# All of x transposed by TensorE in a hybrid attention encoder, with its first eight steps written out by hand

## The chip, the core and the metric

One core of one Trainium2 chip runs the whole layer. The metric is the device time of one execution in microseconds (us); the time given for a kernel is the median of its runs.

## What is computed

One layer for x of 1024 tokens by 1024 features, float32: a root-mean-square norm, one projection to 3328 columns, two groups of attention heads on its parts, a gate for each, an output projection, the residual, and a final norm. Cut to what matters:

```python
h = _rmsnorm(x, norm_gain[l])
proj = h @ w_in[l]
q_a, k_a, v_a, g_a, q_b, k_b, v_b, g_b = jnp.split(proj, split_at, axis=-1)
q_a = _rmsnorm(q_a.reshape(b, s, A_HEADS, HEAD_DIM), q_norm_a[l])      # 8 heads of 64
k_a = _rmsnorm(k_a.reshape(b, s, A_KV_HEADS, HEAD_DIM), k_norm_a[l])   # 2 heads
q_a = q_a * cos + _rotate_half_axial(q_a) * sin
k_a = k_a * cos + _rotate_half_axial(k_a) * sin
o_a = _gqa_blocked(q_a, k_a, v_a) * jax.nn.silu(g_a)      # softmax over all 1024 keys
o_b = _neighbourhood_attn(q_b, k_b, v_b, na_rpb[l]) * jax.nn.silu(g_b)   # window 8 x 16 of the 16 x 64 grid
x = x + jnp.concatenate([o_a, o_b], axis=-1) @ w_out[l]
return _rmsnorm(x, final_norm_gain)
```

## The kernel before

**Precision.** The matrix products run in float16, each operand split into a high part and the rest (hi and lo), and three products are summed: hi·hi, hi·lo, lo·hi. So each projection of one tile of 128 tokens to 256 columns has 8 chunks of the contraction times 3, 24 matmuls.

**The work on PE.** The tokens are 8 tiles (u = 0 to 7). The columns are groups of 256: group 0 (KVA) is K and V of head group A, 1 and 2 (QA) are its Q, 3 to 12 the rest, 13 to 16 the output projection. `proj_pair` (L511) makes the projection of one group for two tiles, a *pair* of 48 matmuls in 8 *chunks* of 6; its left operand comes from hT, the transposed x, in hi (`hT[0]`) and lo (`hT[1]`). Nine pairs come before the first score of group A, in the order K0 Q0 K1 Q1 K2 K3 Q2 Q3 (each number is two tiles) and the first of group 2. Then 64 *units* follow, one for each Q tile and head: scores (L741, L743), their softmax on DVE and ACT (L748, L752, L753, L758), a DMA transpose of the probabilities (L763), and five units later the product with V (L775, L776). The projections still to be done fill PE between, at 5.0 chunks a unit for the first four units and 4.2 for the next seven. Group B's attention and the output projection come behind.

**How x gets into hT.** For each tile: `load_x` (L234) brings it in, into one of four buffers; `x_sq` (L298) sums its squares on ACT (the last on DVE); `x_rs` (L308) makes the scale (DVE, then two operations on POOL); `x_y` (L314) scales it on DVE and copies it on ACT to float16 (the hi part), and `x_lo` (L319) subtracts, on DVE (once on POOL), for the lo part. `x_t` (L323) sends each part through a DMA transpose on SP's queue, so there are 16. For each weight, `prep_a` sums squares, `prep_b` (L382) makes a scale with a small matmul, `prep_c` (L394, ACT) and `prep_d` (L399, DVE) split it; weights from group 3 on are split in quarters (`split`, L408, lines 414 and 419).

**What sets the order.** PE's order is the program's own. The other engines have their order written out by hand in the first part of the program (up to the first `fl.step`); behind it, up to the seventh unit, a scheduler orders them, and then by hand again. `Flow` is a clock of steps: `at(delay, pos, fn)` puts work at a position of a later step, `run(pos)` does what is due there, and `step(n)` runs "pre", "mid" and "post" and then lets PE do n chunks (8 before the first unit). After a pair is projected, `norm_rope` (L537) does its norm and rotation in three pieces: a (ACT, two evacuations of PSUM, L550 and L551), b (DVE sum, POOL power), c (DVE and POOL, the rotation; lines 560 to 568); then `fin` splits the result into hi (ACT) and lo (DVE), and a DMA transpose puts it into kTa and klo1 (K) or qTa (Q).

Of the kernel before, what the change touches and what calls it, by code (L numbers as in the profile page):

```python
# [8 lines left out]
F32 = mybir.dt.float32  # L9
F16 = mybir.dt.float16  # L10
BF16 = mybir.dt.bfloat16
AF = mybir.ActivationFunctionType
# [20 lines left out]
X2_BEHIND = {0: (0, 1), 1: (2,), 2: (3,), 3: (4,), 4: (5,), 5: (6,), 6: (7,)}  # L33
PREP = {2: 4, 3: 0, 4: 2}
NEG = -1.0e37
# [12 lines left out]
class Flow:  # L48
# [78 lines left out]
    def step(self, n, first=None, second=None, last=None):  # L127
        if self.base:
            us = self.base[0] + 0.654 * n
            self.budget = {"act": us - self.base[1], "dve": us - self.base[2]}  # L130
        self.run("pre")
        self.work("act", self.early)
        if first:
            first()
        if self.early is not None:
            self.tail = self.slot
            self.work("act", more=True)
            self.tail = -1
        if second:
            second()  # L140
        self.run("mid")
        self.work("dve")
        self.run("post")
        self.fill(n)
        if last:
            last()
        self.run("end")
        self.slot += 1
# [3 lines left out]
def kernel(ctx: ExitStack, tc: tile.TileContext, x: bass.AP, w: bass.AP, wo: bass.AP,  # L152
# [161 lines left out]
    def x_y(u):  # L314
        dve.scalar_tensor_tensor(xts[u], xts[u], xr[u][:, 1:], gain, op0=OP.mult, op1=OP.mult)
        act.activation(xhl[u][:, 0], xts[u], AF.Copy)
        x_t(u, 0)

    def x_lo(u, e):  # L319
        e.tensor_tensor(xhl[u][:, 1], xts[u], xhl[u][:, 0], op=OP.subtract)  # L320
        x_t(u, 1)
# [71 lines left out]

    def prep_c(g):  # L394
        for i in range(0, KC, KC // 2):
            s = slice(i, i + KC // 2)
            act.activation(wp[g][0][:, s], raw[g][:, s], AF.Copy, scale=col(S_ + g))
# [68 lines left out]
    def prep(g):  # L466
        if g < 3:
            d = PREP.get(g, 1)
            at(d + 1, "pre", prep_a, g)
            at(d + 2, "mid", pend.append, g)  # L470
        else:
            want.add(g)
            try_split(g)
# [61 lines left out]
    klo1 = carve(rq, 16384, [NU, P], F16)  # L535

    def norm_rope(g, up, src, nh, kq, done):  # L537
        n = 2 * nh
# [30 lines left out]

        at(1, "pre", a)  # L570
        at(1, "post" if g == QA + 1 else "mid", b)
        at(2 if g == QA + 1 else 1, "post", c)
        done(qn)

    def qa_gen(hh, up):
        def evac(pt):
            g = QA + hh
            stg = slot("stg1", [P, 2, 4, P], F16)
            a, b = (0, D) if hh == 0 else (D, 0)

            def fin(q):
                d = 4 if hh else 2
# [6 lines left out]
                at(d, "post", tr)  # L589
            norm_rope(g, up, pt, 4, 0, fin)  # L590
        yield from proj_pair(QA + hh, up, from_h, evac)

    def kva_gen(up):
        def evac(pt):
            both = slot("stg1", [P, 8, P], F16)
            stg, stg_l = both[:, :6].rearrange("p (i a) b -> p i a b", a=3), both[:, 6:]
            vs = pt[:, :, P:].rearrange("p a (h d) -> p a h d", d=D)
            at(1, "pre", lambda: act.activation(va[:, 2 * up:2 * up + 2, :, :D], vs, AF.Copy, scale=2.0 ** -14))
# [5 lines left out]
            at(1, "mid", vlo)  # L604

            def fin(k):
                def hi():
                    act.activation(stg[:, :, :2, :D], k, AF.Copy)
                    act.activation(stg[:, :, :2, D:], k, AF.Copy)
                at(2, "pre", hi)  # L610

                def lo():
                    for h, to in ((0, stg[:, :, 2]), (1, stg_l)):
                        dve.tensor_tensor(to.rearrange("p i (e d) -> p i e d", d=D),
                                          k[:, :, h, None, :].to_broadcast([P, 2, 2, D]),
                                          stg[:, :, h].rearrange("p i (e d) -> p i e d", d=D), op=OP.subtract)
                at(2, "mid", lo)

                def tr():
                    sp.dma_start_transpose(kTa[:, 2 * up:2 * up + 2].rearrange("p i a t -> p (i a) t"),  # L620
                                           both[:, :6].rearrange("p a b -> p (a b)"))
                    sp.dma_start_transpose(klo1[:, 2 * up:2 * up + 2], stg_l.rearrange("p a b -> p (a b)"))
                at(2, "post", tr)
            norm_rope(KVA, up, pt[:, :, :P], 2, 1, fin)
# [440 lines left out]
    with tc.manual_schedule(engines={act.engine, dve.engine, pool.engine, sp.engine}):  # L1065
        x_sq(0, act)
        scale_gain()
        prep_a(0)
        load_w1(2, 3)
        x_rs(0)  # L1070
        x_y(0)
        prep_a2(0)
        prep_b(0)
        x_sq(1, act)
        prep_c(0)
        x_rs(1)
        load_x(2)
        x_lo(0, dve)
        x_y(1)
        load_x(3)  # L1080
        prep_a(1)
        x_lo(1, pool)
        prep_d(0)
        tables_in()
        x_sq(2, act)
        load_x(4)
        x_rs(2)
        load_x(5)
        prep_e(0)
        x_sq(3, act)  # L1090
        x_y(2)
        x_rs(3)
    k, q = [kva_gen(up) for up in UP], group(1, [qa_gen(0, up) for up in UP])
    fl.add(k[0], q[0], k[1], q[1], k[2], k[3], q[2], q[3], *group(2, [qa_gen(1, up) for up in UP]))
    fl.step(PAIR)
    prep_b(1)
    prep_c(1)
    x_y(3)
    x_lo(3, dve)
    x_sq(4, act)  # L1100
    tables()
    scale_tab(2)
    x_rs(4)
    x_y(4)
    x_lo(4, dve)
    x_lo(2, dve)
    x_sq(5, act)
    x_rs(5)
    load_x(6)
    scale_tab(0)  # L1110
    x_y(5)
    prep_d(1)
    x_sq(6, act)
    x_lo(5, dve)
    x_rs(6)
    x_y(6)
    x_lo(6, dve)
    load_x(7)
    scale_tab(3)
    x_sq(7, dve)  # L1120
    prep_e(1)
    gate[2] = 6
    scale_tab(1)
    x_rs(7)
    x_y(7)
    load_w(2)
    gate[3] = 5
    x_lo(7, dve)
    load_w(3)

    for p in range(8):
        fl.step(PAIR)
    fl.add(*group(3, [qb_gen(0, up) for up in UP]))
# [214 lines left out]
```

## Time and profile before

| | |
|---|---|
| time, median of 3 runs | 555.65 us (553.15 to 557.3) |
| profiled execution | 554.79 us, span 553.0 us |
| mean granted clock of TensorE | 0.989 |
| PE busy | 507.8 us, 92% of the span |
| DVE, ACT, POOL busy | 445.3 (81%), 381.4 (69%), 178.9 us (32%) |
| first score matmul (L741) | 87.15 us |
| DMA | 95.40 MB, 173 GB/s; 235,489 of 244,509 packets under 512 B |

The execution's own time holds 1.8 us outside of the span. PE is the engine with the most work; its matmuls are pipelined, so a busy PE need not be at its peak. The profile's slices are 13.8 us each.

### The profile page before, as it was taken

The numbers are of one execution on the slowest core, as the hardware profiler recorded it, in microseconds if no ns is written. First come the engines' busy times: TensorE is split into PE (matmuls) and PEld (weight loads), VectorE is DVE, ScalarE is ACT, GpSimd is POOL, SyncE is SP. The second block draws the span as 40 slices with busy tenths as digits, with TensorE's granted clock in tenths as the row PEclk, the third lists the DMA queues.
The fourth block names the chain that finished last, engine by engine and source line by source line (L and its number), as shares of the span: only waits on it lengthen the run. The fifth ranks groups of instructions, "written<-read, shape, count | busy, mean of one in ns | idle before, by whom it ended". The sixth has DMA issues, their size and how long they took to land.

```text
span 553.0 us, 12864 instructions
## 1 busy us (share of the span) xinstructions
PE 507.8 (92%) x5071; PEld 397.2 (72%) x5071; DVE 445.3 (81%) x887; ACT 381.4 (69%) x671; POOL 178.9 (32%) x201
## 2 busy tenths in 40 slices
PE   2657889998999999999999999999999998799994
PEld 0446768876887555558888888988777786589883
DVE  4599678889987888879879898867898997887732
ACT  4545465967887868787787696648688788784411
POOL 1385787581110000101000022634433123344510
PEclk9989999999999999999999999999999999999998
DMA  8997837879999999999997999744897799979722
GB/s 243 210 203 216 146 59 181 135 144 176 208 196 217 191 231 186 216 176 178 194 217 143 202 186 200 120 125 71 146 191 138 136 250 202 219 115 204 173 74 76
DMA packets 244509, 95.40 MB, mean 173 GB/s; under 512 B 235489, under 2 KB 236001, under 8 KB 242530
## 3 DMA queue, kind: packets, MB, share of 16 engines
q1 hardware_dynamic: 242434, 81.23, 80.1%
q0 software_dynamic: 1728, 12.58, 7.3%
q8 instruction: 39, 0.64, 0.5%
q10 hardware_dynamic: 288, 0.79, 0.5%
q14 instruction: 20, 0.16, 0.1%
HBM read 29.56 MB, written 4.19 MB: 61 GB/s over the span
## 4 chain that ended last, share of the span: by engine, by line
PE 50%; DVE 10%; ACT 9%; issue 5%; DMA 3%; POOL 0%; DVEq 0%; POOLq 0%; ACTq 0%
PE pj L504 17%; PE kb L504 7%; PE pjb L504 7%; PE pv L775 5%; PE s L741 4%; PE s L743 4%; ACT rq L856 3%; DVE ar L854 3%; ACT ar L858 2%; PE pv L776 2%; PE sb L504 2%; DMA pt<-ar 2%; DVE ar L863 1%; DMA ar<-ar 1%; DVE whl L419 1%
## 5 line engine op out<-in xcount | busy, mean ns | idle before, releaser
L504 PEld LDWEIGHTS <-hT 128*128 128x128 f16 x2112 | 204.2, 99 | 59.5 <-DMA hT<-ar 16.3
L504 PE MATMUL pj<-whl,hT 128*128 128x256 f16 x1680 | 201.7, 278 | 21.8 <-DMA hT<-ar 9.4
L752 ACT ACTIVATE ar<-s,nm,sm 128x1024 f32<-128x1024 f32 x64 | 76.9, 1201 | 47.7 <-DVE nm L748 45.7
L748 DVE CUSTOM_DVE_ANT_0 ar<-s,sm 128x1024 bf16<-128x1024 f32 x64 | 82.0, 1281 | 30.3 <-PE s L743 28.5
L504 PEld LDWEIGHTS <-ar 128*128 128x128 f16 x768 | 73.8, 98 | 16.0 <-issue 7.8
L758 DVE TENSOR_TENSOR ar<-ar 128x1024 f16<-128x1024 f32 x64 | 79.4, 1241 | 1.2 <-ACT ar L753 1.2
L753 ACT ACTIVATE ar<-ar 128x1024 f16<-128x1024 f32 x64 | 67.6, 1057 | 2.3 <-DVE ar L758 0.4
L504 PE MATMUL pjb<-whl,ar 128*128 128x256 f16 x480 | 56.4, 273 | 2.8 <-ACT whl L414 1.5
L856 ACT ACTIVATE rq<-ar,nm 128x384 f32<-128x384 f32 (+1 forms) x64 | 34.0, 579 | 25.7 <-DVE nm L854 25.1
L504 PE MATMUL pjb<-whl,hT 128*128 128x256 f16 x432 | 50.4, 273 | 0.1
L784 POOL TENSOR_TENSOR ar<-ar,sum 128x256 f32<-128x256 f32 x16 | 11.3, 709 | 110.7 <-DVE ar L783 95.3
L504 PE MATMUL kb<-hT,whl 128*128 128x512 f16 x192 | 44.5, 379 | 0.0
L419 DVE SCALAR_TENSOR_TENSOR whl<-raw,sm,whl 128x512 f16<-128x512 f32 x52 | 41.0, 821 | 2.7 <-ACT whl L414 2.7
L775 PE MATMUL pv<-va,ar 128*128 128x128 f16 x384 | 39.1, 220 | 0.0
L863 DVE SCALAR_TENSOR_TENSOR ar<-rq,ar 128x768 f16<-128x768 f32 (+1 forms) x32 | 29.3, 915 | 11.0 <-ACT ar L858 10.6
L741 PE MATMUL s<-kTa,rq 128*128 128x512 f16 x128 | 38.1, 379 | 0.0
L776 PE MATMUL pv<-va,ar 128*128 128x64 f16 x384 | 37.8, 193 | 0.0
L775 PEld LDWEIGHTS <-ar 128*128 128x128 f16 x384 | 33.9, 98 | 5.3
L776 PEld LDWEIGHTS <-ar 128*128 128x128 f16 x384 | 33.2, 98 | 5.3
L414 ACT ACTIVATE whl<-raw,sm 128x512 f16<-128x512 f32 x52 | 34.0, 709 | 1.4 <-POOL sm L391 1.4
L391 POOL TENSOR_TENSOR sm<-wss,mh 128x1 f32<-128x1 f32 x17 | 10.5, 619 | 72.7 <-DVE wss L390 72.7
L910 POOL TENSOR_TENSOR ar<-ar,qkg 128x256 f32<-128x256 f32 x16 | 17.1, 1072 | 51.6 <-DVE qkg L908 36.4
(174 smaller groups left out, 915.9 us busy)
## 6 DMA issues: line engine op xcount, KB each, us to landing
raw<-in_w_dram POOLq DMA_DIRECT2D x11, 1024.0 KB, 7.6
ar<-in_x_dram SPq DMA_DIRECT2D x7, 512.0 KB, 6.1
raw<-in_wo_dram SPq DMA_DIRECT2D x3, 1024.0 KB, 7.0
khh<-ar SPq DMA_DIRECT2D x16, 128.0 KB, 2.7
x2b<-in_x_dram SPq DMA_DIRECT2D x4, 512.0 KB, 7.4
x<-in_x_dram SPq DMA_DIRECT2D x4, 512.0 KB, 5.6
out_dram<-x2b SPq DMA_DIRECT2D x8, 256.0 KB, 4.1
out_dram<-x SPq DMA_DIRECT2D x7, 256.0 KB, 2.9
```

The source lines that it names most:

```text
L414: act.activation(wp[g][0][:, q], raw[g][:, q], AF.Copy, scale=col(S_ + g))
L419: dve.scalar_tensor_tensor(wp[g][1][:, q], raw[g][:, q], col(S_ + g), wp[g][0][:, q], op0=OP.mult, op1=OP.subtract)
L504: pe.matmul(*o[0], **o[1])
L741: pe.matmul(s[:, c * 512:(c + 1) * 512], q, kTa[:, 4 * c:4 * c + 4, hh], start=True, stop=False)
L748: dve.tensor_tensor_reduce(out=hl[:, 1].bitcast(BF16), in0=s, in1=col(SHA).to_broadcast([P, 1024]), scale=col(NSA), scalar=3e38, op0=OP.ad ...
L752: act.activation(p32, s, AF.Exp, bias=nm, scale=col(SCA), accum_out=rsum[hh, u][:, h:h + 1])
L753: at(0, "mid", lambda: act.activation(hl[:, 0], p32, AF.Copy))
L758: dve.tensor_tensor(hl[:, 1], p32, hl[:, 0], op=OP.subtract)
L775: pe.matmul(o, pt[:, kt], va[:, kt, hh], start=kt == 0, stop=False)
L776: pe.matmul(o[:, :D], pt[:, 8 + kt], va[:, kt, hh, :D], start=False, stop=kt == 7)
L856: act.activation(p32[:, e], t[:, e], AF.Exp, bias=nm, scale=-1.0)
L863: dve.scalar_tensor_tensor(hl[:, 1], p32, 2.0 ** 14, hl[:, 0], op0=OP.mult, op1=OP.subtract)
```

## The change

Five things change.

1. **x is transposed by TensorE.** `x_scale` scales a tile on DVE; `tp` transposes its eight blocks of 128x128 in float32 with `pe.transpose` against an identity (made by POOL), all into one PSUM tile xT (two banks, made once, used by all eight x tiles); `tp_hi` copies each half to `hT[0]` on ACT, `tp_lo` subtracts on DVE to `hT[1]`. The 16 DMA transposes are gone.
2. **20 matmuls with no use** (`busy`) go before the first transpose.
3. **The first eight steps are by hand**, on all engines: `stage(i)` names what runs before, between and after PE's chunks. `norm_rope` and the evacuations use positions of their own ("a", "v", "b").
4. **The rotations are spread.** Piece c and what follows come later by `lag`: for the K pairs 3, 2, 1, 0 steps, for group 1's Q 3, 3, 1, 1, for group 2's 1 to 4. All of K is rotated in steps 4 to 6.
5. **Weight loads 2 to 4 go to SP** (before: POOL), the load of group 4, the fifth, after the K transposes of step 7.

The core of the diff:

```diff
-        (sp if "b" in late else pool).dma_start(raw[g], w[g] if g < 13 else wo[g - 13])
+        (sp if "b" in late or g < 5 else pool).dma_start(raw[g], w[g] if g < 13 else wo[g - 13])
...
+    ident = carve(ar, MIX + 2048, [P], F32)
+    pool.memset(ident, 1.0)
+    pool.affine_select(out=ident, in_=ident, pattern=[[-1, P]], compare_op=OP.is_equal, fill=0.0, base=0,
+                       channel_multiplier=1)
...
+    def x_scale(u):
+        dve.scalar_tensor_tensor(xts[u], xts[u], xr[u][:, 1:], gain, op0=OP.mult, op1=OP.mult)
...
+    def tp(u, *ks):
+        if not xT:
+            xT.append(ps_s.tile([P, KC, P], F32, tag="s", name="xT"))
+        for k in ks:
+            pe.transpose(xT[0][:, k], xts[u][:, k * P:(k + 1) * P], ident)
+
+    def tp_hi(u, half):
+        ks = slice(4 * half, 4 * half + 4)
+        act.activation(hT[0][:, ks, u * P:(u + 1) * P], xT[0][:, ks], AF.Copy)
+
+    def tp_lo(u):
+        cs = slice(u * P, (u + 1) * P)
+        dve.tensor_tensor(hT[1][:, :, cs], xT[0], hT[0][:, :, cs], op=OP.subtract)
+
+    def busy(n):
+        b = ident.bitcast(BF16)
+        for _ in range(n):
+            pe.matmul(spare[0][:, :256], b[:, :P], b, start=True, stop=True)
...
+    def lag(g, up):
+        return {KVA: (3, 2, 1, 0), QA: (3, 3, 1, 1), QA + 1: (1, 2, 3, 4)}[g][up]
...
-        at(1, "pre", a)
-        at(1, "post" if g == QA + 1 else "mid", b)
-        at(2 if g == QA + 1 else 1, "post", c)
+        at(1, "a", a)
+        at(1, "post" if g == QA + 1 else "b", b)
+        at(1 + lag(g, up), "post", c)
...
         x_rs(0)
-        x_y(0)
+        x_scale(0)
+        busy(20)
+        tp(0, 0, 1, 2)
         prep_a2(0)
         prep_b(0)
+        tp(0, *range(3, 8))
         x_sq(1, act)
-        prep_c(0)
+        load_x(4)
+        tp_hi(0, 0)
+        prep_c(0, (0,))
         x_rs(1)
...
+            if i == 1:
+                yield "a v"
+                yield 2
+                tp(2, *range(8))
+                load_x(6)
+                load_w(3)
+                split_t(2)
+                x_sq(4, act)
...
+            if i == 7:
+                yield "a v pre mid"
+                load_w(4)
+                yield "b post"
+                yield 8
```

`split_t(u)` is the two `tp_hi` and `tp_lo`; a number that a stage yields is that many chunks on PE. Steps 2 to 5 have the tiles 3 to 7 in the same way, with 36 matmuls of PE between one tile's transposes and the next one's.

**PE, from its start to the first projection.** hT_99 and hT_101 are the hi part of hT, whl the split weight of group 0, wss its sum of squares, pv a spare PSUM tile, ar the large working store in which x lies. Before:

```order
L242 MATMUL gain_p<-gain_i,ar 128x512 x2
L388 LDWEIGHTS mh
L388 MATMUL pv_101<-wss_118,mh 128x1
L504 LDWEIGHTS hT_99
L504 MATMUL pj_0_177<-whl_117,hT_99 128x256
```

Now (the twenty pairs of a load and a matmul in front are shown once):

```order
L349 LDWEIGHTS ar
L349 MATMUL pv_104<-ar 128x256
L336 MATMUL xT<-ar 128x128 x3
L422 LDWEIGHTS mh
L422 MATMUL pv_103<-wss_120,mh 128x1
L336 MATMUL xT<-ar 128x128 x5
L536 LDWEIGHTS hT_101
L536 MATMUL pj_0_177<-whl_119,hT_101 128x256
```

The transposes (L336) stand around the weight's sum, and the next tile's eight stand six projection matmuls further on.

**SP's queue behind the first weight loads.** L236 and L242 load x, L273 and L275 (L279, L281) the tables of the rotation, L223 a weight, L620, L622, L655 and L657 transpose K, L587 and L622 (after) Q. Before:

```order
L324 DMA_TRANSPOSE hT_99<-ar 128x8x128
L236 DMA ar<-in_x_dram 128x1x1024
L324 DMA_TRANSPOSE hT_100<-ar 128x8x128
L324 DMA_TRANSPOSE hT_99<-ar 128x8x128
L236 DMA ar<-in_x_dram 128x1x1024
L324 DMA_TRANSPOSE hT_100<-ar 128x8x128
L273 DMA qkg<-in_qk_gain_dram 128x256
L275 DMA tabs<-in_rope_dram 128x512 x2
L236 DMA ar<-in_x_dram 128x1x1024 x2
```

Now:

```order
L242 DMA ar<-in_x_dram 128x1x1024 x4
L279 DMA qkg<-in_qk_gain_dram 128x256
L281 DMA tabs<-in_rope_dram 128x512 x2
L223 DMA raw_220<-in_w_dram 128x2048
L242 DMA ar<-in_x_dram 128x1x1024
L223 DMA raw_296<-in_w_dram 128x2048
L242 DMA ar<-in_x_dram 128x1x1024
L655 DMA_TRANSPOSE kTa<-ar 128x6x128
L657 DMA_TRANSPOSE rq<-ar 128x2x128
```

The loads of x follow each other, two weight loads stand among them, and the first transposes on the queue are K's.

**The first score, on DVE and ACT.** On DVE, L748 and L783 are the first operation on a score tile, L584 and L619 the lo part of a Q pair, L560 and L567 (L595, L602) the rotation, L419 and L455 a quarter of a weight's split. Before:

```order
L419 SCALAR_TENSOR_TENSOR whl_817<-raw_310,sm,whl_817 128x512 x2
L584 TENSOR_TENSOR ar<-ar 128x8x64
L560 TENSOR_TENSOR ar<-ar,nt_3_794 128x512
L567 TENSOR_TENSOR ar<-ar,tabs 128x512
L748 ISA ar,nm_0_0_886<-s_0_0_881,sm 128x1024
L748 ISA nm_0_0_886 128x1
```

Now, from the first score on:

```order
L783 ISA ar,nm_0_0_953<-s_0_0_948,sm 128x1024
L783 ISA nm_0_0_953 128x1
L589 TENSOR_REDUCE nt_0_944<-ar 128x8
L595 TENSOR_TENSOR ar<-ar,nt_3_876 128x512
L590 TENSOR_SCALAR nt_0_944<-nt_0_944,sm 128x8
L424 TENSOR_SCALAR wss_0_298<-pv_103 128x1
L602 TENSOR_TENSOR ar<-ar,tabs 128x512
```

The rotation of the last Q pair of group 1 (nt_3), which stood ahead of the first score, is behind it; so are two of the three Q subtractions that were ahead, and the split of the weight of group 3, which now comes between the third and the fourth score.

On ACT at the same place, L643 and L644 are the hi copies of a K pair, L585 and L586 (L550, L551 before) the evacuation of a Q pair. Now:

```order
L433 ACTIVATE whl_739<-raw_220,sm 128x1024 x2
L585 ACTIVATE ar<-pj_2_749 128x512
L586 ACTIVATE ar<-pj_2_749 128x512
L643 ACTIVATE ar<-ar 128x2x2x64
L644 ACTIVATE ar<-ar 128x2x2x64
L643 ACTIVATE ar<-ar 128x2x2x64
L644 ACTIVATE ar<-ar 128x2x2x64
L585 ACTIVATE ar<-pj_3_827 128x512
```

and before, where L608 and L609 are the same copies:

```order
L608 ACTIVATE ar<-ar 128x2x2x64
L609 ACTIVATE ar<-ar 128x2x2x64
L550 ACTIVATE ar<-pj_2_670 128x512
L551 ACTIVATE ar<-pj_2_670 128x512
L608 ACTIVATE ar<-ar 128x2x2x64
L609 ACTIVATE ar<-ar 128x2x2x64
L397 ACTIVATE whl_648<-raw_305,sm 128x1024 x2
```

The copies of the last two K pairs now both stand behind the evacuation of the third Q pair; before, one of them did.

More of the change, by code (lines that the diff above doesn't have):

```diff
@@ L140, in step @@
             second()
+        self.run("v")
         self.run("mid")
@@ L143, in step @@
         self.run("post")
+        self.run("b")
         self.fill(n)
@@ L392, in prep_b, with prep_c @@
         scaled.add(g)
-    def prep_c(g):
-        for i in range(0, KC, KC // 2):
+    def prep_c(g, halves=(0, 1)):
+        if g not in wp:
+            alloc_wp(g)
+        for i in [KC // 2 * h for h in halves]:
             s = slice(i, i + KC // 2)
@@ L1084 @@
+        tp_hi(0, 1)
+        prep_c(0, (1,))
+        tp_lo(0)
+        prep_d(0)
+        k, q = [kva_gen(up) for up in UP], group(1, [qa_gen(0, up) for up in UP])
+        fl.add(k[0], q[0], k[1], q[1], k[2], k[3], q[2], q[3], *group(2, [qa_gen(1, up) for up in UP]))
+        fl.fill(1)
+        prep_a(1)
+        tp(1, *range(8))
+        fl.fill(3)
+        load_x(5)
+        tp_hi(1, 0)
+        tp_hi(1, 1)
+        tp_lo(1)
         tables_in()
+        load_w(2)
+        prep_b(1)
+        fl.fill(4)
@@ L1085 @@
         x_sq(2, act)
[L1086 removed]
         x_rs(2)
[L1088 to L1089 removed]
+        prep_c(1)
+        x_scale(2)
+        prep_d(1)
         x_sq(3, act)
[L1091 removed]
         x_rs(3)
[L1093 to L1101 removed]
@@ L1102, with split_t @@
[L1102 to L1132, printed above, removed]
+        def split_t(u):
+            tp_hi(u, 0)
+            tp_hi(u, 1)
+            tp_lo(u)
@@ new lines, with q_sq, stage @@
+        wss[2] = [tn(f"wss2_{k}", 1, "ws") for k in range(4)]
+        def q_sq(*qs):
+            for i in qs:
+                act.activation(va_more.rearrange("p (k c) -> p k c", c=GC), raw[2][:, QUARTERS[i]], AF.Square,
+                               accum_out=wss[2][i])
+        def stage(i):
+            if i == 1:
[6 more added lines that the diff above has]
+                x_sq(4, act)
+                x_rs(4)
+                x_scale(3)
+                x_sq(5, act)
+                x_rs(5)
+                prep_e(0)
+                yield "b"
+                x_scale(4)
+                yield 6
+            if i == 2:
+                tp(3, *range(8))
+                yield "a"
+                load_x(7)
+                split_t(3)
+                prep_e(1)
+                x_scale(5)
+                yield "b"
+                q_sq(0, 1)
+                yield 6
+                tp(4, *range(8))
+                split_t(4)
+                x_sq(6, act)
+                x_rs(6)
+                tables()
+                scale_tab(2)
+                scale_tab(3)
+                yield 2
+            if i == 3:
+                yield "a v b"
+                q_sq(2, 3)
+                x_scale(6)
+                yield 4
+                tp(5, *range(8))
+                split_t(5)
+                x_sq(7, act)
+                x_rs(7)
+                prep_b(2)
+                scale_tab(0)
+                scale_tab(1)
+                yield 4
+            if i == 4:
+                yield "a b"
+                x_scale(7)
+                yield 2
+                tp(6, *range(8))
+                split_t(6)
+                yield "post"
+                yield 6
+            if i == 5:
+                tp(7, *range(8))
+                yield "a v"
+                split_t(7)
+                yield "post pre mid b"
+                yield 8
+            if i == 6:
+                yield "a v b post pre mid"
+                prep_c(2)
+                prep_d(2)
+                yield 8
+            if i == 7:
+                yield "a v pre mid"
+                load_w(4)
+                yield "b post"
+                yield 8
@@ L1133 @@
+        for i in range(1, 8):
+            fl.slot += 1
+            for todo in stage(i):
+                if isinstance(todo, int):
+                    fl.fill(todo)
+                else:
+                    for pos in todo.split():
+                        fl.run(pos)
+            fl.run("end")
+        fl.slot += 1
+    fl.step(PAIR)
     fl.add(*group(3, [qb_gen(0, up) for up in UP]))
```

35 lines of the change are left out of this document (16 added, 19 removed).

## The prediction

> **What bounds the kernel now.** I read the shares of the page first, then its forty slices of 13.8 us, then the chain that ended last, then the PE timeline at the start.
>
> ```profile
> PE 507.8 (92%) x5071; PEld 397.2 (72%) x5071; DVE 445.3 (81%) x887; ACT 381.4 (69%) x671; POOL 178.9 (32%) x201
> PE   2657889998999999999999999999999998799994
> DVE  4599678889987888879879898867898997887732
> DMA  8997837879999999999997999744897799979722
> 137.18 1.97 PE pj L504 x18
> 341.07 2.62 PE pj L504 x24
> 365.31 2.15 DVE rq L797 x2
> ```
>
> PE is the fullest engine, and its only long loss is in the first six slices. In the chain, PE stands alone from 137 to 345 us; from 365 DVE and ACT take over, in work that the change doesn't touch. So what PE gains before it is saturated moves everything behind it by as much. That stretch by stage (columns: length; PE, PEld, DVE, ACT, POOL busy; clock, DMA share, GB/s):
>
> ```profile
> 0.00:14.60 14.60, 3.91 (x5) 1.26 (x5) 5.79 (x11) 7.32 (x10) 3.09 (x10) 1.00 0.81 235
> 14.60:87.20 72.60, 55.68 (x439) 45.54 (x440) 56.84 (x115) 38.48 (x69) 50.83 (x56) 0.95 0.80 169
> 69.75 5.40 PE L504 MATMUL pj<-whl,hT 128*128 128x256 f16 x48
> 74.99 0.17 PE L388 MATMUL pv<-wss,mh 128*128 128x1 bf16 x1
> 87.15 0.59 PE L741 MATMUL s<-kTa,rq 128*128 128x512 f16 x2
> PEld L504 <- DMA hT<-ar: 16.3, 4, 8.5
> PE pj L504 <- DMA hT<-ar: 9.4, 4, 3.1
> PE pj L504 <- ACT whl L397: 6.7, 2, 5.5
> hT<-ar SPq DMA_TRANSPOSE x16, 4.6
> ```
>
> The first score matmul is at 87.15. Until then PE has nine pairs of 48 projection matmuls. One undisturbed pair takes 74.99 - 69.75 = 5.24 us, 0.1092 each, so 432 need 47.2 of the 72.6 us: **25 us are waiting**, and the waits name it, mostly DMA transposes into hT (the PEld and PE rows overlap, so they aren't added), then the weights of ACT. This is the stage to be priced.
>
> **The change part by part.**
>
> *Removed*: the 16 transposes into hT on SP's queue (4.6 us each from issue to landing), their waits, and the copies' detour through xhl. What is late next is worked out below.
>
> *Added on PE*: 64 transposes of 128x128 float32 and 20 warming matmuls. No float32 transpose is in this trace. The nearest rows are the gain broadcast, also float32:
>
> ```profile
> L242 PEld LDWEIGHTS gain_p<-gain_i,ar x4: 280/330/332, 2.4 to 4.2; 1*128 1x128 f32 x4
> L242 PE MATMUL gain_p<-gain_i,ar x4: 1056/1056/1185, 2.4 to 5.1; 1*128 1x512 f32 x4
> 108.05 0.22 PE L775 MATMUL pv<-va,ar 128*128 128x128 f16 x1
> 108.13 0.22 PE L775 MATMUL pv<-va,ar 128*128 128x128 f16 x1
> ```
>
> Four matmuls of 512 columns start within 2.7 us, 0.90 apart: 0.225 us for 128 columns, the loads beside them. From below, f16 matmuls of 128 and of 64 columns alternate within 0.08 us, so 0.055 each; from above, a load of 0.33 and then 0.225, so 0.555. I take **0.225**, the row of the same type. The warming matmuls stand between the gain's end (6.15) and x's first scaled tile (10.57, below); at 0.2 each, 4 us, they fit, if the identity from POOL is there; if it came 3 us late, it would cost up to 3.
>
> *The same work elsewhere*: ACT's 8 copies of 1024 become 16 of 512 read from PSUM, DVE subtracts 8 times from PSUM instead of 7 times from SBUF (one was POOL's), and a sum of squares goes from DVE to ACT.
>
> ```profile
> 9.29 1.28 DVE L315 SCALAR_TENSOR_TENSOR ar<-ar,xs,gain_p 128x1024 f32<-128x1024 f32 x1 [1.01 <-POOL xs L312]
> 11.82 0.16 PE L388 MATMUL pv<-wss,mh 128*128 128x1 bf16 x1 [5.68 <-DVE wss L379]
> 17.12 1.89 ACT L359 ACTIVATE whl<-raw 128x2048 bf16<-128x2048 f32 x1
> L550 ACT ACTIVATE ar<-pj 128x512 f32<-128x512 f32 x8 | 4.7, 585 | 4.5 <-PE pj L504 4.5
> L320 DVE TENSOR_TENSOR ar<-ar 128x1024 f16<-128x1024 f32 x7 | 9.0, 1283 | 0.0
> 15.98 2.34 DVE L404 SCALAR_TENSOR_TENSOR whl<-raw,sm,whl 128x2048 f16<-128x2048 f32 x1
> ```
>
> *The first pair*: x0 is scaled at 10.57. Three transposes, the sum for the weight scale (to 11.98), five more: 13.1. DVE scales x1 behind that (about 13.6 to 14.9), subtracts x0 to 16.2 and splits the weight to 18.5. The second x tile must wait for the one PSUM tile xT until 16.2, is transposed by 18.0, copied by 19.1 (ACT is in the 1.89 us of squares until 17.5) and subtracted by 20.4. The last 16 of the 48 matmuls need that: the pair ends at **22.2**.
>
> *The other eight pairs*: 384 x 0.1092 = 41.9, and 48 transposes x 0.225 = 10.8, if each tile is ready when PE reaches it. Between two tiles PE has 36 matmuls (54 the first time), 3.9 us, and the loop from a tile's last transpose to the next one's first is one copy of 0.585 behind the first, and 1.28 on DVE, about 2.5 with a wait between: covered. The first score matmul then comes at 22.2 + 41.9 + 10.8 = **74.9**.
>
> *K rotated late or early*: kTa must be whole by then. ACT's copies for the last K pairs stand behind the evacuation of the seventh pair, which ends at 74.9 - 2 x 5.24 = 64.4.
>
> ```profile
> L608 ACT ACTIVATE ar<-ar 128x256 f16<-128x256 f32 x4 | 1.7, 419 | 2.3 <-POOL ar L568 2.3
> L614 DVE TENSOR_TENSOR ar<-ar 128x256 f16<-128x256 f32 x8 | 3.0, 416 | 1.2 <-ACT ar L609 1.2
> 76.97 1.21 SPq L620 DMA_TRANSPOSE kTa<-ar  x1
> rq<-ar SPq DMA_TRANSPOSE x11, 3.4
> ```
>
> Two evacuations (1.2), four copies (1.7) and two subtractions (0.8) give 68.1; three issues of 1.2 before the last, and 3.4 for its landing: 75.1. That is 0.2 behind PE, so nothing is hidden there: what DVE or POOL lose shows at once. Rows of DVE beside a busy POOL differ by a quarter for one shape:
>
> ```profile
> L560 DVE TENSOR_TENSOR ar<-ar,nt 128x512 f32<-128x512 f32 x8 | 5.5, 688 | 1.9 <-POOL nt L556 1.8
> L567 DVE TENSOR_TENSOR ar<-ar,tabs 128x512 f32<-128x512 f32 x8 | 6.8, 855 | 0.1
> L556 POOL TENSOR_TENSOR nt<-nt,mh 128x4 f32<-128x4 f32 x4 | 5.4, 1348 | 0.6 <-DVE nt L555 0.5
> L568 POOL TENSOR_TENSOR ar<-ar 128x256 f32<-128x256 f32 x4 | 2.9, 724 | 0.2
> ```
>
> POOL's power and addition are 2.1 us a K pair; with its two products and DVE's five rows of 0.4 to 0.8 it is about 6, so 12 for the last two pairs. Nothing to a quarter of that is 0 to 3; I take the upper end, since POOL has these rotations back to back: **78**.
>
> *Weight loads on SP*: loads 2, 3 and 4 leave POOL's queue. SP's issue of the fifth load (group 4) waits for the third weight to be split, with Q transposes queued behind it; of these the ones for the fifth Q tile on are read only from the 17th score unit. I cost it at nothing; without that cover it would be the wait for the split, 2.3 us by L404's row.
>
> *What moves behind the first score*: of three Q pairs' last subtraction, two are now after it on DVE, with one rotation and the whole split of weight 3.
>
> ```profile
> 87.00:104.00 17.00, 17.00 (x141) 13.61 (x140) 13.91 (x19) 14.17 (x31) 11.49 (x10) 1.00 0.70 142
> 104.00:121.00 17.00, 17.00 (x177) 13.66 (x176) 15.43 (x23) 13.35 (x21) 12.24 (x9) 1.00 1.03 176
> 121.00:138.00 17.00, 14.77 (x160) 11.91 (x156) 16.96 (x31) 11.96 (x19) 5.09 (x5) 1.00 0.93 152
> L419 DVE SCALAR_TENSOR_TENSOR whl<-raw,sm,whl 128x512 f16<-128x512 f32 x52 | 41.0, 821 | 2.7 <-ACT whl L414 2.7
> ```
>
> Four splits of 0.82, two subtractions of about 0.7 and a rotation of 1.4 are 6.1 us. DVE has 17 - 13.91 = 3.1 us free in the first stretch and 1.6 in the second, and in the third it was full already and cost PE 2.2. 6.1 - 4.7 = 1.4 doesn't fit: I take **2** lost, between 0 (some of it runs while DVE waits for the first score) and 6.
>
> *Sum*: 87.15 - 78 = 9.2 earlier, less 2: 7.2. The profiled execution took 554.79 (span 553.0 and 1.8 around it), so 547.6; the median of the three runs, 555.65, is 0.86 higher: **548**.
>
> **The rivals.** *No change: transposes at half clock.*
>
> ```profile
> 30.00:40.00 10.00, 6.73 (x45) 5.11 (x45) 9.17 (x19) 5.42 (x8) 10.00 (x9) 0.83 1.12 205
> 14.64 1.89 PE L504 MATMUL pj<-whl,hT 128*128 128x256 f16 x8 [2.65 <-DMA hT<-ar]
> ```
>
> After waits the granted clock drops (0.83 in this stretch), and the first eight matmuls took 0.24 each, twice the later 0.109. If transposes ran unoverlapped at about twice the 0.225, 0.45, the 56 from the second tile on would add 56 x 0.225 = 12.6, and the score would come at 87.5 (kTa hidden by it) to 90.6: with 2 lost, 558 to 561. For it: nothing says that such matmuls keep the clock up; against: each batch of eight stands between 36 others. The Trainium skill's page "TensorE: Matmul & The Clock Gate", part 4 on PE-mode transpose, says that transpose mode doesn't count as busy for the full clock, and gives about 275 ns in one kernel: by that estimate 64 would cost 17.6 us, 2.8 more than here costed over the last 56. No run here shows it yet.
>
> *Slower: one xT tile in lockstep.* Each tile waits for DVE's subtraction of the one before, with all of PE behind it, and ACT's copies and that subtraction stand behind squares, evacuations and scalings. The loop of 2.5 us has 1.4 to spare. It runs for six tiles, so each us beyond the spare costs 6: 1.3 takes the whole gain, 2.2 makes it slower by 1%, and 3 gives 548 + 18 = 566. Against: ACT was busy 38 of 72.6 us there, so it seldom has a queue.
>
> *Little change: DVE is the bound of the start.* It was busy 5.8 + 56.8 us to the score; 6.1 of that go behind it, 56.5 stay. If it idles as before, 24.6 us, the score comes at 81, and with 2 lost the gain is 4: 551.6. For it: in the second stretch DVE is as full as PE. Against: part of that idling was for the same transposes.
>
> *More than forecast*: transposes overlapped, 0.11 each, save 6.4, with no stretch and nothing lost behind: 548 - 11 at most, so 537 to 543.
>
> **How the numbers follow.** Forecast 0.45 (544 to 551), more 0.15, DVE 0.13, half clock 0.15, lockstep 0.12. The range 541 to 560 leaves out the lower half of "more" and most of lockstep. Faster by over 1%, under 550.1, is most of the forecast (0.39), all of "more" and a little of the DVE case: 0.56; within 1%, about what a measurement of this kernel can tell from no change: 0.32; slower: 0.12.
>
> **What would show it.** No hT row among the DMA transposes; transposes at L336 about 0.225 apart; the first pair ended near 22; the first score (L776) near 78; PE waits for kTa at the score under 3 us; DVE nearly full for 50 us behind it and PE losing 4 us there instead of 2. I am wrong if PE waits at L336 for more than 1 us per tile, if the score comes after 83, or if the time to the score is gained and DVE gives it back.

## The result and the profile after

The changed kernel takes **552.04 us** (median of 6 runs, 551.26 to 552.81) where the kernel before takes 556.27 on the same chip (6 runs): a ratio of 0.9932, 95% interval 0.9903 to 0.9961, so 4.2 us or 0.7% off. I had forecast 548 from 555.65. The sign was right and the size was not. The profiled execution has a span of 551.1 us against 553.0: 1.9 of the 4.2 us, since the one that was profiled before (554.79) is among the faster ones of its kernel. (All ratios leave out runs in which the chip granted a lower clock and the medians don't, so where the two disagree below, go by the ratio.)

The page of the changed kernel, shares and slices:

```profile
PE 517.7 (94%) x5158; PEld 407.7 (74%) x5158; DVE 446.1 (81%) x886; ACT 382.9 (69%) x687; POOL 167.5 (30%) x197
PE   6999989299999999999999999999999998799994
```

The start is full now (before: 265788). But there is a new hole, the 2 in the eighth slice, 96 to 110 us. By stage (length; PE, PEld, DVE, ACT, POOL busy; clock, DMA share, GB/s), the changed kernel:

```profile
0.00:14.60 14.60, 9.62 (x35) 5.26 (x36) 5.61 (x11) 6.67 (x11) 2.74 (x12) 0.96 0.88 254
14.60:87.20 72.60, 69.40 (x589) 59.41 (x587) 61.66 (x117) 46.08 (x98) 44.11 (x52) 0.94 0.42 108
87.20:155.30 68.10, 57.05 (x566) 46.01 (x564) 59.68 (x104) 51.62 (x90) 25.76 (x22) 0.92 0.94 172
```

and the last of these stretches in the kernel before:

```profile
87.20:155.30 68.10, 65.87 (x655) 53.27 (x653) 63.13 (x104) 55.09 (x95) 30.44 (x25) 1.00 0.95 169
```

Up to 87.2 PE is busy 13.7 us more in the second stretch (69.40 against 55.68). In the next it is busy 8.8 us less, and DVE 3.5 us less: neither is the limit there. The PE timeline of the changed kernel shows where:

```profile
25.18 1.04 PE L336 MATMUL xT<-ar 128*128 128x128 f32 x8
71.64 0.38 PE L776 MATMUL s<-kTa,rq 128*128 128x512 f16 x1
74.40 0.39 PE L776 MATMUL s<-kTa,rq 128*128 128x512 f16 x1 [2.38 <-DMA kTa<-ar]
98.28 0.59 PE L776 MATMUL s<-kTa,rq 128*128 128x512 f16 x2 [1.13 <-ACT ar L787]
108.50 0.27 PE L810 MATMUL pv<-va,ar 128*128 128x128 f16 x1 [9.20 <-DMA ar<-ar]
```

The first score comes at 71.64, and goes on at 74.40 when kTa is whole: 12.8 us ahead of 87.15. Then the product of unit 0 with V starts at 108.50, after 9.2 us of waiting for the transposed probabilities (P). Before, it started at 108.05 without a wait. **Nearly all of the head start is gone at that one row.** The two queues of SP, first before, then after the change:

```profile
86.62 10.82 SPq L587 DMA_TRANSPOSE rq<-ar  x2
97.58 7.03 SPq L763 DMA_TRANSPOSE ar<-ar  x2
```

```profile
85.70 11.26 SPq L622 DMA_TRANSPOSE rq<-ar  x2
97.05 5.44 SPq L798 DMA_TRANSPOSE ar<-ar  x1
102.59 1.26 SPq L622 DMA_TRANSPOSE rq<-ar  x1
103.90 4.52 SPq L798 DMA_TRANSPOSE ar<-ar  x2
```

Which pair and which unit a row belongs to follows from the stores that the built program reads and writes there. Before, the rows are Q pairs 2 and 3, then the P of units 0 and 1. After, they are Q pairs 1 and 3, the P of unit 1, Q pair 2, and the P of units 0 and 2: the scheduler has put pair 3 and unit 1 ahead of pair 2 and unit 0. So unit 0's transpose of P (L763, now L798) is issued at 103.90 in place of 97.58, though its score was there 13 us earlier and DVE ended the subtraction of its P (L793) at 85.06. It landed at 108.36, and the product started at 108.50. What the queue waits for ahead of it, by its waits and DVE's timeline:

```profile
SPq L622 <- DVE ar L619: 10.9, 1, 10.9
```

```profile
83.83 1.23 DVE L793 TENSOR_TENSOR ar<-ar 128x1024 f16<-128x1024 f32 x1
91.35 3.74 DVE L455 SCALAR_TENSOR_TENSOR whl<-raw,sm,whl 128x512 f16<-128x512 f32 x4
95.01 0.68 DVE L619 TENSOR_TENSOR ar<-ar 128x512 f16<-128x512 f32 x1
97.41 1.28 DVE L619 TENSOR_TENSOR ar<-ar 128x512 f16<-128x512 f32 x2
```

Q pair 3's subtraction (95.01), for which the 10.9 us are waited, and Q pair 2's (the first at 97.41) stand behind all four quarters of weight 3's split; in the kernel before, pair 2's came at 85.92. The P of unit 1 then holds the queue for 5.44 us. There is also a reason in the stores why the P of unit 0 can't overtake Q pair 2: the transposed P of units 0, 1 and 2 goes into `ar` at 22,528, 26,624 and 30,720, and Q pairs 1 to 3 are rotated at 20,480 to 32,767. Unit 0's lies over pairs 1 and 2, unit 1's over 2 and 3.

### The profile page after: what moved, and what is told of

The parts are those of the page before. It is cut to its first block, busy times and chain, and to the rows that moved or that the text cites. A ratio compares the mean times of both kernels' runs of the same rounds, so it can differ in the third digit from the quotient of the medians.

```text
span 551.1 us, 13028 instructions
## 1 busy us (share of the span) xinstructions
PE 517.7 (94%) x5158; PEld 407.7 (74%) x5158; DVE 446.1 (81%) x886; ACT 382.9 (69%) x687; POOL 167.5 (30%) x197
## 4 chain that ended last, share of the span: by engine, by line
PE 64%; ACT 11%; DVE 11%; issue 6%; DMA 4%; POOL 3%; DVEq 0%; POOLq 0%; ACTq 0%; SPq 0%
PE pj L536 26%; PE pjb L536 8%; PE kb L536 8%; PE pv L810 5%; PE s L776 5%; PE s L778 5%; ACT rq L891 4%; PE pv L811 3%; ACT ar L893 3%; DMA ar<-ar 2%; PE sb L536 2%; DVE ar L889 2%; DVE whl L455 1%; POOL nt L591 1%; PE xT L336 1%
## 5 line engine op out<-in xcount | busy, mean ns | idle before, releaser
L536 PE MATMUL pj<-whl,hT 128*128 128x256 f16 x1680 | 199.5, 276 | 3.3 <-ACT whl L433 2.2
L783 DVE CUSTOM_DVE_ANT_0 ar<-s,sm 128x1024 bf16<-128x1024 f32 x64 | 82.0, 1281 | 36.1 <-PE s L778 32.2
L793 DVE TENSOR_TENSOR ar<-ar 128x1024 f16<-128x1024 f32 x64 | 78.7, 1230 | 1.2 <-ACT ar L788 1.1
L455 DVE SCALAR_TENSOR_TENSOR whl<-raw,sm,whl 128x512 f16<-128x512 f32 x52 | 41.1, 826 | 2.7 <-ACT whl L450 2.7
L819 POOL TENSOR_TENSOR ar<-ar,sum 128x256 f32<-128x256 f32 x16 | 10.9, 681 | 106.1 <-DVE ar L818 90.7
L898 DVE SCALAR_TENSOR_TENSOR ar<-rq,ar 128x768 f16<-128x768 f32 (+1 forms) x32 | 30.0, 937 | 10.9 <-ACT ar L893 10.6
```

The costliest lines, as they stand in the source:

```text
L455: dve.scalar_tensor_tensor(wp[g][1][:, q], raw[g][:, q], col(S_ + g), wp[g][0][:, q], op0=OP.mult, op1=OP.subtract)
L536: pe.matmul(*o[0], **o[1])
L783: dve.tensor_tensor_reduce(out=hl[:, 1].bitcast(BF16), in0=s, in1=col(SHA).to_broadcast([P, 1024]), scale=col(NSA), scalar=3e38, op0=OP.ad ...
L793: dve.tensor_tensor(hl[:, 1], p32, hl[:, 0], op=OP.subtract)
L898: dve.scalar_tensor_tensor(hl[:, 1], p32, 2.0 ** 14, hl[:, 0], op0=OP.mult, op1=OP.subtract)
```

## Experiments

The theories that the expectations name. **A**: the gain of the start is lost in a chain of waits, from the rotation of Q pairs 1 and 2 by way of the free store and SP's order to the first transposes of P and the product with V. **B**: the 1 MB load of weight 5, issued at 95.40 beside the first of these transposes, holds them up. **C**: DVE's sum of work sets the pace after the first score, in whatever order. **D**: each us of PE ahead of the first score moves the end, as I had summed it. "Before" is timed beside each group of runs.

### Other stores for unit 0's and unit 1's transposed P

```diff
-        if i % 4 == 3:
+        if i % 4 == 1:
             pt = one.tile([P, 16, P], F16, tag="gain", name=f"pt{hh}_{u}_{h}")
         else:
-            pt = carve(ar, 4096 * RING + 2048 + 4096 * (i % 4), [16, P], F16)
+            pt = carve(ar, 4096 * RING + 2048 + 4096 * (0, 0, 2, 1)[i % 4] if i else MIX, [16, P], F16)
```

> Unit 0's and unit 1's transposed probabilities go into stores that no Q pair uses (mixA's first, free until unit 8, and the gain's tile), so that the first P transpose need not wait for Q pairs 1 to 3 and stands ahead of their transposes in SP's queue. Theory A (the 9.2 us wait at unit 0's product with V is the chain Q rotation, free store and SP's order, first P transpose): the first P transpose is issued near 84 in place of 97.05, the wait for it falls from 9.2 us to under 3, and the time from 552.0 to 545-549. Theory B (the 1 MB weight load beside the first P transposes makes them long): these now run ahead of that load, so it gains too; the run with a later load tells. Theory C (DVE's sum of work in the stretch sets the pace, in whatever order): the wait goes from L810 to the scores, the time stays within 1.5 us of 552.

545.31 us, ratio 0.9809 (0.9758 to 0.986). It ran again, for a profile to lay beside the changed kernel's:

> The kernel with unit 0's and unit 1's transposed probabilities in stores that no Q pair uses, once more, for a profile that can be laid beside the changed kernel's and a closer time. Theory A: the first score stays where it is (its first matmul near 71.6, its second near 74.4), the first P transpose is issued 10 us or more ahead of 97.05, the 9.2 us wait at unit 0's product with V is under 2 us, and TensorE's busy time between 87.2 and 155.3 rises from 57.05 to 64 us or more. Theory C: the wait is found again at the scores or the pairs.

**543.94 us, ratio 0.9786 (0.9757 to 0.9816).** Its PE timeline, SP queue, and the stretch behind the score:

```profile
71.08 0.38 PE L776 MATMUL s<-kTa,rq 128*128 128x512 f16 x1
73.86 0.39 PE L776 MATMUL s<-kTa,rq 128*128 128x512 f16 x1 [2.39 <-DMA kTa<-ar]
107.83 0.22 PE L810 MATMUL pv<-va,ar 128*128 128x128 f16 x1 [1.12 <-DMA ar<-ar]
```

```profile
84.28 1.80 SPq L798 DMA_TRANSPOSE ar<-ar  x1
86.17 1.85 SPq L622 DMA_TRANSPOSE rq<-ar  x1
```

```profile
87.20:155.30 68.10, 63.76 (x654) 51.07 (x652) 66.37 (x116) 56.08 (x96) 27.82 (x25) 1.00 1.07 188
```

The first score is where it was, unit 0's transpose of P is issued at 84.28 in place of 103.90 and ahead of Q pair 1's, and the only wait of a product with V is now 1.1 us, at a later unit. PE is busy 63.76 us in the stretch in place of 57.05; I had said 64 or more. DVE, at 59.68 in the changed kernel, does 66.37 in the same 68.1 us, so it had room: theory A, against C. Eight us came back with no work removed. Unit 0's P is now also clear of the load of weight 5, so this run can't tell how much of the eight is theory B's.

### The same stores in the kernel before

The edit is the one above.

> The same two stores given to the kernel before the change. Theory A: there unit 0's product with V at 108.05 did not wait, since its score came 15.5 us later and the first P transpose (97.58) was soon enough; the stores bring it nothing: 555-557. Then the change itself, with the stores, is worth 10-12 us, and the P stores hid most of it. Rival: the stores cost both kernels the same; then this run gains 6 us too (550) and the change is worth 4 us whatever the stores.

555.12 us, ratio 0.999 (0.9959 to 1.002): nothing. The stores alone are worth nothing where the first score comes at 87, and the change with them is worth 2.1% (0.9786), 12 us. So the change is worth about what its head start was (12.8 us at the first score), and with the old stores two thirds of that were lost.

### The load of weight 5 later

```diff
-                at(1, "pre", load_w, g + 2)
+                at(5 if g == 3 else 1, "pre", load_w, g + 2)
```

> The load of weight 5 (1 MB from POOL, issued at 95.40 beside the first P transposes) is put off by four units. Theory B (the load stretches the first P transpose, 5.44 us from issue to landing): the transpose lands in 2.5-3.5 us and the wait at unit 0's product with V falls by 2-3 us, the time to about 549.5. Theory A: the issue at 97.05 stays where it is, the transpose itself may gain up to 2 us, the wait stays over 7 us, the time within 1 us of 552.

551.63 us, ratio 0.9926 (0.9901 to 0.995). The edit didn't move the load. It is issued at 94.88, against 95.40 in the changed kernel, in the same order on POOL, and the PE wait is still there:

```profile
94.88 0.79 POOL L223 DMA_DIRECT2D raw<-in_w_dram  x1 [2.85 <-DVE whl L455]
PE pv L810 <- DMA ar<-ar: 9.3, 1, 9.3
```

So **theory B is not tested** by this run. In the changed kernel the load lasts from 95.40 to 101.70, and the P of unit 1 beside it held SP's queue for 5.44 us, where with the other stores the P of unit 0, clear of a load, held it for 1.80. By these two rows B could be worth up to 3.6 us of the 9.2 (an estimate); it stays open.

### Q pairs 1 and 2 rotated a step earlier

```diff
-        return {KVA: (3, 2, 1, 0), QA: (3, 3, 1, 1), QA + 1: (1, 2, 3, 4)}[g][up]
+        return {KVA: (3, 2, 1, 0), QA: (3, 2, 0, 1), QA + 1: (1, 2, 3, 4)}[g][up]
```

> Q pairs 1 and 2 are rotated one step earlier (steps 2 and 0 after their sums in place of 3 and 1; the rest as it is). Theory A: Q pair 2's subtraction on DVE ends near 90 in place of 95.7, the first P transpose starts 3-6 us earlier, the wait of 9.2 us shrinks by as much, and the time goes to 547-550. But the earlier rotation takes DVE time from K's pairs: if these come later by more than 1 us, the first score does too. Theory C (DVE's work in sum, not its order): within 1.5 us of 552.

550.57 us, ratio 0.9904 (0.987 to 0.9937), a smaller gain than I expected of A and not clear of the changed kernel's 0.9932. Unit 0's transpose of P is issued at 90.52 in place of 103.90, and the wait at unit 0 is gone from PE's list:

```profile
90.52 2.19 SPq L798 DMA_TRANSPOSE ar<-ar  x1
```

But K's pairs came later by the work put ahead of them:

```profile
75.95 0.38 PE L776 MATMUL s<-kTa,rq 128*128 128x512 f16 x1
```

```profile
PE s L776 <- DMA kTa<-ar: 3.1, 1, 3.1
```

The score's first matmul moved from 71.64 to 75.95, and it goes on 3.1 us behind that. What the Q pairs gain by a place in the order, K loses. The stores take the wait away without moving any work.

### Transposes of tiles 2 to 7 issued twice

```diff
-            pe.transpose(xT[0][:, k], xts[u][:, k * P:(k + 1) * P], ident)
+            for _ in range(2 if u > 1 else 1):
+                pe.transpose(xT[0][:, k], xts[u][:, k * P:(k + 1) * P], ident)
```

> The transposes of x tiles 2 to 7 are issued twice each: 48 more on TensorE ahead of the scores, 5.2 us at the 0.109 us that eight of them took at full clock. Theory A: the first score comes up to 5 us later, the wait of 9.2 us at unit 0's product with V shrinks by as much (to about 4-6 us), and the time moves by under 1.5 us (552 to 553.5). Theory D (each us of TensorE's work ahead of the first score moves the end): 557. If a transpose costs the 0.273 us of its record instead of 0.109, the first score comes 13 us later and the time is past 556 by either.

559.68 us, ratio 1.0058 (1.0026 to 1.009): 7 us worse than the change alone. **My expectation from theory A failed**, and D's was nearly right. The waits for P are no shorter:

```profile
PE pv L811 <- DMA ar<-ar: 11.6, 2, 9.1
```

I had taken the 9.2 us for slack up to a fixed time. It isn't one: Q pairs 2 and 3 are among the last pairs that PE makes before the scores, so when PE is late, the chain behind them is late by nearly as much: the first score by 4.3 us, unit 0's transpose of P by 3.6 (107.47). A holds for where the wait is from, not for its being a cushion. With the stores:

> The two stores that no Q pair uses, and the transposes of x tiles 2 to 7 issued twice each (48 more on TensorE). In the run with the doubling alone the wait of 9.1 us at unit 0's product with V stayed and the time rose by 7.6 us. With the wait gone, what is left is the price of a transpose on TensorE: 5.2 us at 0.109 each, so 550.5; if each cost the 0.225 that the prediction took, 10.8 us and 556; if the doubling only shifts work into idle time of TensorE, 545-547.

551.4 us, ratio 0.9933 (0.9904 to 0.9963), about 8 us above the run with the stores alone. Its PE timeline:

```profile
25.02 1.91 PE L337 MATMUL xT<-ar 128*128 128x128 f32 x16
76.66 0.38 PE L777 MATMUL s<-kTa,rq 128*128 128x512 f16 x1
```

Sixteen transposes in 1.91 us against eight in 1.04: 0.109 each. The score moves from 71.08 to 76.66, 5.6 us, as 48 x 0.109 + 0.4. In these two profiles the score of unit 14 is 5.3 us later (143.58 against 138.27). The median moves by 2 us more than that; PE waits 3.3 us for ACT's exponentials at the scores there (2.2 with the stores alone), and the rest I can't name.

### Half of x by DMA as before

```diff
-                tp(4, *range(8))
-                split_t(4)
+                x_hi(4)
+                x_lo(4, pool)
...
```

and so for tiles 5, 6 and 7.

> The x tiles 4 to 7 go into hT as before the change (rounded on ACT, the remainder on POOL, two DMA transposes each), tiles 0 to 3 by TensorE, all else as in the changed kernel. By the rows of before, where PE waited 25.7 us for sixteen such transposes, half of them cost up to 13 us of waits less the 3.5 us of 32 transposes on TensorE: the first score at 78-84 in place of 71.6. Theory A: the P transpose at 97 is set by the Q pairs, which come later by less than the score, so the wait of 9.2 us shrinks, and the time is 553-557. Theory D: all of the delay moves the end, 559-563.

554.22 us, ratio 0.9967 (0.9942 to 0.9993). Half of the transposes undone takes back about half of the gain (0.9932); the time is in the range of theory A. I read the ratio alone here, not the waits. (The 25.7 us in the expectation adds two rows of waits that overlap.)

### The fifth weight load back on POOL

```diff
-        (sp if "b" in late or g < 5 else pool).dma_start(
+        (sp if "b" in late or g < 4 else pool).dma_start(
```

> The part of the change that puts the fifth weight load on SP undone: it goes from POOL's queue again. The prediction priced it at nothing. If SP's queue held it back (it is issued near 85 behind K's last transposes there) or it holds back the Q transposes behind it, the first P transpose moves by up to 1 us; if POOL has to wait for the load's store with Q's rotations behind it, Q pairs 1 to 3 come later and the time rises by up to 3 us. Expected: within 1.5 us of 552.

547.62 us, ratio 0.9837 (0.9798 to 0.9876): **4.4 us better than the whole change** by the medians (5.3 by the ratios), a surprise for a part that I had priced at nothing. DVE's timeline and SP's queue:

```profile
89.77 0.75 DVE L455 SCALAR_TENSOR_TENSOR whl<-raw,sm,whl 128x512 f16<-128x512 f32 x1
90.44 1.77 DVE L619 TENSOR_TENSOR ar<-ar 128x512 f16<-128x512 f32 x1
92.13 2.07 DVE L455 SCALAR_TENSOR_TENSOR whl<-raw,sm,whl 128x512 f16<-128x512 f32 x3
```

```profile
85.63 7.83 SPq L622 DMA_TRANSPOSE rq<-ar  x2
93.56 1.64 SPq L798 DMA_TRANSPOSE ar<-ar  x1
```

Up to unit 6 a scheduler orders ACT, DVE, POOL and SP. With the load elsewhere it wrote another order: Q pair 2's subtraction stands ahead of three quarters of weight 3's split, at 90.44 in place of 97.41, and unit 0's transpose of P is issued at 93.56 in place of 103.90. To tell this order from the queue itself, two kernels have all units in the program's own order (`HAND = 0` in place of 6), and differ only in the queue of that load:

> All of the units stand in the program's own order (the scheduler orders none of the first six). The reference for the next run: the first P transpose is behind Q pairs 1 and 2 on SP as in the changed kernel, so the wait at unit 0's product with V should be near 9 us and the time within 3 us of 552.

> The same order on TensorE, DVE and ACT as in the run before, and the fifth weight load on POOL in place of SP: nothing else differs. If the queue makes the 4.4 us, this run is 3 us or more below that one. If it was the order that the scheduler wrote (theory A: the place of Q pair 2's subtraction before the first P transpose), the two are within 1.5 us of one another.

Ratios 0.9932 (0.9902 to 0.9962) and 0.9935 (0.9895 to 0.9975): the same. In this order the queue costs nothing, as I had priced it. In the changed kernel the load took SP's queue for 0.57 us at 74.13 (not near 85, as I had written), long before the next transpose at 85.70. So I put the 4.4 us down to the **order** that came with the load; the better order with the load on SP was not run, so this last step is argued. And with the stores, where the wait is gone already, the load on POOL brings nothing more:

> The P stores that no Q pair uses, and the fifth weight load on POOL. Theory A: both edits take away the same wait (the first P transpose behind the Q pairs), so the time is that of the stores alone, 543-546, or up to 2 us above, since with the load on POOL the second unit's score came 2.7 us later. If the load on SP has a cost of its own, the gains add: 539.5.

543.51 us, ratio 0.9767 (0.9718 to 0.9816), against 0.9786 for the stores alone. So the two edits take away the same wait.

In the written order the wait isn't where I expected it. Its PE waits:

```profile
PE s L776 <- ACT ar L787: 8.7, 3, 4.4
```

No product with V waits (unit 0's P is issued at 92.94), but three scores wait 8.7 us for exponentials. The same order with the stores:

> The P stores that no Q pair uses, in the program's own order: SP has the transposes of Q pairs 1 and 2 ahead of the first P transpose, as in the changed kernel, though its store is free. If the store holds the first P transpose back, the time is near 544-546 as with the scheduler's order; if SP's order does, since Q pair 2's transpose waits there for DVE, the transpose comes after 90, the wait at the product with V is 4 us or more, and the time 548-552.

552.82 us, ratio 0.9946 (0.9908 to 0.9985). The stores bring nothing here: the time is just above the range that I had given to SP's order, and the wait at the product with V that belongs to it isn't there. SP still has both Q transposes ahead, and the scores wait as above, for DVE has Q's subtractions ahead of the units' own work and stands at them until ACT has Q's halves:

```profile
81.29 6.23 SPq L622 DMA_TRANSPOSE rq<-ar  x2
91.44 2.01 SPq L798 DMA_TRANSPOSE ar<-ar  x1
```

```profile
PE s L776 <- ACT ar L787: 8.6, 4, 4.5
```

```profile
80.18 1.08 DVE L619 TENSOR_TENSOR ar<-ar 128x512 f16<-128x512 f32 x1 [3.59 <-ACT ar L618]
85.57 0.69 DVE L619 TENSOR_TENSOR ar<-ar 128x512 f16<-128x512 f32 x1 [4.30 <-ACT ar L618]
```

So a free store isn't enough; the order has to use it. As later scores are late here, this run doesn't tell SP's queue from DVE's order, and that stays open.

### A store of its own for Q pair 0's staged halves

With the P stores ACT waits 4.2 us in K pair 2's copies (L643) for Q pair 0's transpose, whose staging buffer they take. In the changed kernel:

```profile
67.41 0.42 ACT L643 ACTIVATE ar<-ar 128x256 f16<-128x256 f32 x1 [4.56 <-DMA rq<-ar]
```

```diff
-            stg = slot("stg1", [P, 2, 4, P], F16)
+            stg = slot("stg1", [P, 2, 4, P], F16) if hh + up else carve(ar, MIX + 6144, [2, 4, P], F16)
```

Alone, with the P stores, and with the split of weight 3 held back besides (`delay=4 if g == 3 else 1` on its ACT jobs):

> The changed kernel with a store of its own for Q pair 0's staged halves, and the P stores as they were. Theory A: the first score's second matmul comes about 2.4 us earlier, but unit 0's product with V still waits for the first P transpose, which is tied to the Q pairs: the wait of 9.2 us grows by that much or stays tied to them, and the time stays within 1.5 us of 552. Theory D (each us up to the first score moves the end): 549.6.

> Besides the P stores of the runs before, Q pair 0's staged halves get a store of their own, so that K pair 2's halves on ACT need not wait for Q pair 0's DMA transpose (4.2 us, L643 waiting for DMA rq). Theory A: K's last transpose lands 2-4 us earlier, the 2.4 us wait for kTa at the second matmul of the first score goes, and the time falls from 543.9 by about 2.4, to 541-542.5. Rival (TensorE's other work and DVE fill that hole anyway, the wait comes back at ACT's exponentials): 543-545.

> Both kinds of stores as in the other run of this call, and the split of weight 3 (ACT 2.55 us, DVE 3.74 us between the scores of the first units) put off by three units. If these splits hold back the exponentials on which the scores wait (2.2 us in two places), the time falls by 1-2 us below the run with the stores alone (540-541.5); Theory C (DVE's sum of work counts, not its order): the same as that run within 1 us; if the weight is then late for its pairs, TensorE waits for whl and the time rises by 1-4 us.

Ratios 0.9917 (0.9889 to 0.9945), 0.9788 (0.9757 to 0.982) and 0.9784 (0.9745 to 0.9822): none differs from the run without it. ACT and DVE with both stores say why:

```profile
62.33 0.42 ACT L643 ACTIVATE ar<-ar 128x256 f16<-128x256 f32 x1 [0.23 <-POOL ar L603]
68.03 0.42 ACT L643 ACTIVATE ar<-ar 128x256 f16<-128x256 f32 x1 [4.98 <-DMA kTa<-ar]
```

```profile
63.95 2.94 DVE L440 SCALAR_TENSOR_TENSOR whl<-raw,sm,whl 128x1024 f16<-128x1024 f32 x2
```

ACT's wait went from K pair 2 to pair 3 (4.98 us, for the transpose of an earlier K pair, whose staging buffer pair 3 takes), and DVE is in weight 2's split (2.94 us) before it subtracts K pair 2. K's last transpose is issued at 70.80, against 71.00 with the P stores alone, and the wait at kTa is 2.4 us as it was. My expectation of 2.4 us was a wait read without what stood behind it on the next engine.

The best version is the change with the P stores: 543.9 us, 2.1% under the kernel before and 1.5% under the changed one. The three others at 543.5 to 544.4 can't be told from it.

## Why the prediction was right and wrong

- **25 us of waiting in the start, and the end moves with the score.** Right about where: the hole was in the start, and with the P stores 12.8 us at the first score became 12 us at the end by the ratio (9.4 by the two spans, 543.6 and 553.0). The doubled transposes show the same from the other side. One reading was wrong: in the chain, PE isn't alone from 137 to 345; a DMA piece of 9.27 us stands at 163.32.
- **Transposes at 0.225.** Too dear by half: 0.109 in the row at 25.18. That is 5.6 us of the 10.8 for 48 of them, and my "more than forecast" case (0.11) had it right. The gain broadcast is no measure for a transpose of the same type. Only tile 1's batch was as dear as I had costed, 0.21 apart (eight in 1.91 us at 16.14), at a granted clock of 0.50.
- **First pair at 22.2.** It ended near 23.9 (the last 24 of its matmuls start at 21.04); the clock was not yet full (18 matmuls in 3.33 us at 17.84; granted clock 0.62 from 18 to 21). This took back 1.7 us.
- **Score by PE at 74.9, kTa at 75.1, 3 us of stretch: 78.** PE was there at 71.64, kTa at 74.40. That kTa landed near 75.1 was luck, two errors that cancel. The evacuation of the seventh pair began at 61.80, where I had 64.4 for the pair's end, and then ACT waited 4.56 us in K pair 2's copies for Q pair 0's transpose, whose staging buffer they take. I had no term for that wait. The 3 us of stretch on top didn't show, so 12.8 us were gained where I had 9.2.
- **"What moves behind the first score", priced at 2 us of DVE. This is the step that failed.** I counted 6.1 us of work into DVE's free time. What it cost was no capacity: DVE was busy 3.5 us *less* in the stretch. Q pair 2's subtraction, one of those I had counted, moved from 85.92 to 97.41, and by SP's order and by the store unit 0's transpose of P comes behind it. I never asked what waits for the work that I moved. The runs showed that chain in its place: the transpose is issued at 103.90, though its input was there at 85.06, the product with V stays at 108, and hardly anything of 12.8 us is left by unit 14 (147.09 now, 147.41 before, in these profiles).
- **Weight load on SP, nothing.** Right for the queue in a fixed order (0.9932 and 0.9935), wrong for the kernel: with the load elsewhere the scheduler orders the first six units in another way, and the two kernels differ by 4.4 us.
- **Half clock.** The Trainium skill's page "TensorE: Matmul & The Clock Gate", Part 4 on PE-mode transpose, gives about 275 ns for one. The records are 273 ns long, so they agree in length; the pace is 0.109, since they overlap. Its remark that the full clock doesn't engage for transposes is not borne out between matmuls: eight followed one another at 0.109, at a granted clock of 1.00 (25 to 27 us). Whether transposes alone raise the clock, no run here shows. The drop of the clock that the rival feared met the transposes once: PE waited 1.72 us before 14.23, the granted clock was 0.50 from 14.2 to 18.0, and tile 1's transposes, at 16.14, fell into it.
- **Lockstep on xT.** Didn't happen: all waits at L336 were under 1 us in sum per cause, while ACT and DVE kept up with every tile. **DVE the bound of the start** would have the score at 81; it didn't come about.
- **"I am wrong if the time to the score is gained and DVE gives it back."** It was gained and given back, by the order on DVE and SP, not by DVE's fullness.

## What to carry to other kernels

When work is moved behind a milestone, don't ask only whether its engine has the time; ask who waits for each piece, and what shares its queue and its store. A gain that vanishes at one row (here a product waiting 9.2 us) is read backward from that row: the transfer, the queue's order, the instruction that the queue waited for, what stood ahead of that. Name each row by the store that it reads and writes: of two like transposes here, the later one was the one waited for. Look in the profile whether an edit moved what it was to move; the load of weight 5 stayed where it was. Where a scheduler writes the order, an edit that costs nothing by itself can still be worth more than the one beside it, so compare the written orders, and test the edit in a fixed one.

## What the runs showed of the hardware

- A float32 transpose of 128x128 on TensorE keeps the pace of an f16 matmul of 256 columns: 0.109 us between starts at a granted clock of 1.00 (0.21 at 0.50), with a weight load of 0.141 us beside it, though the float32 matmuls of the gain's broadcast took 0.225 us per 128 columns.
- After the wait of 9.2 us, the sixteen matmuls of a product with V took 1.25 us (108.50 to 109.75), against 0.68 in the kernel before without a wait. The granted clock was 0.50 from 108.50 to 112.00, against 1.00 there, so the wait cost some 1.7 us more than its length (an estimate: half of 3.5 us).
